# Hybrid decode step: memory values by tokens, norm weights on ScalarE, a shorter Newton step, selected-value loads one per step

## The chip, the core and the metric

The kernel runs on one core of a Trainium2 chip, as one launch. The metric is the device time of that launch in microseconds (us). Beside it stands the profile of one execution, taken by the hardware profiler. The core has five engines with a queue of instructions each: TensorE (PE; its weight loads are shown as PEld), VectorE (DVE), ScalarE (ACT), GpSimd (POOL) and SyncE (SP), which here only issues DMA transfers. GpSimd issues DMA transfers too, in the same queue as its arithmetic. An engine takes its own queue strictly in order; between engines, semaphores hold an instruction until its inputs are there and its output buffer is free.

## The reference

One layer of a decoder step over 256 prompt tokens and 8 × 4 = 32 decode tokens (288 columns in all), width 2048, float32:

```python
h = rms_norm(x, norm_g)                       # x * rsqrt(mean(x^2) + eps) * g
c_h, c_b, c_c, c_g, q, n_g, b_g, kv6, m_q, m_g = split_cols(h @ w_in)
y_a = silu(c_g) * short_conv(c_h, c_b, c_c)   # 512 channels
y_b = silu(n_g) * (g0 * o_cmp + g1 * o_sel + g2 * o_win)   # 8 heads, compressed / selected / window
mkv = rms_norm(mem_prompt, mem_norm_g) @ w_mem_kv          # 256 memory tokens: keys, values of 4 heads
y_m = silu(m_g) * attend(m_q, mkv or cache_mem)
y = rms_norm(x + concat(y_a, y_b, y_m) @ w_out, final_g)
```

The decode tokens attend to a paged cache of 2048 positions, of which the compressed branch picks 16 blocks of 64. Outputs are y, the new keys and values, the window and convolution states, and the memory keys and values.

## The kernel before, in words

**Layout.** Activations stand with channels on the 128 partitions and tokens along the free axis: x as 16 planes of 128 × 288, the memory prompt as 16 planes of 128 × 256. A product of the projections is 128 output channels by all tokens. Its weights come in two *halves*, tiles of 128 × 1024 (eight k-blocks of 128). For precision, weights and activations are each split into a high part (fp32r, by a ScalarE copy, `w_hi`) and a low part (what is left, by a VectorE subtraction, `w_lo`), and a half takes 24 matmuls: high × high, high × low, low × high for eight blocks (`product_half`, line 250). Halves are numbered `s`: 0 to 15 the memory projection, 16 to 119 `w_in`, and then `w_out`. At the start of half `s` the code puts `w_hi(s + 2)` on ScalarE and `w_lo(s + 1)` on VectorE; at matmul 21 of the half it issues the weight load of half `s + 6` (on GpSimd's queue from half 14) and, early on, one of the six loads of x (`x_next`).

**Order.** The order of work is written out by the program. All side work is Python generators in a list; after every 12 matmuls `chunk()` (line 161) advances each generator that is due by one step, so that its instructions are put in the queues between those matmuls. A generator yields the number of steps it wants to rest. A planner keeps an estimated clock for each engine (`at`) and uses it to hold work back (`until`, `ready`, `BACKLOG`); it only decides the order. `stages` (line 717) lists the cache work with due times in steps, `load_next` (line 731) fills six buffers of 128 × 1024 with the next loads on that list whenever buffers come free, and `stage_stream` uses them.

**Memory projection (22.5 to 60.7 us).** Tiles 0 to 3 are keys, 4 to 7 values, one tile per head. `mem_tile` (line 1016) brings a tile out of its result buffer: the keys by ScalarE, the values by VectorE times the token norm `rstd_m`, which is spread over all partitions. The result buffers are two (`pz`). Attention over the memory wants the values with tokens on the partitions, so `mem_rstd` (line 878) then transposes each value tile (two transposes on TensorE), copies both out by ScalarE and writes the tile to `o_mem`.

**x.** `prep_x` (line 930) multiplies each of 16 planes by the norm weight `g` (per partition) and the token factor `r` in one VectorE operation, three planes at a time; then ScalarE rounds the three planes to the high part and VectorE subtracts the low part. The x products, from half 16 on, need the parts.

**Selected values.** `selv_load` (line 583) fetches 128 rows of the value cache by an indirect DMA on GpSimd's queue. A stage (`selv_use`) takes four of them; there are eight stages, four for each half of the decode batch. `load_next` issues the loads as soon as buffers are free, up to four in a row. GpSimd's other work is half of the product of the compression (`cmp_use`, line 350): VectorE multiplies the key half of a tile, GpSimd the value half once VectorE's is done, and VectorE sums both later (`pooled`).

**Memory part of the output projection.** `split_y1` (line 1390) splits the mixed activations for `w_out`; it asks at each step whether the decode tokens' memory attention is there (`mem_decoded`), and splits that part then.

**Tail.** The last four column blocks of the output are computed with tokens on the partitions: two groups of 128 prompt tokens (`z[0]`, `z[1]`) and the 32 decode tokens (`zd`, `decode_rows`). For each group `squares` adds the residual on VectorE and sums the squares on ScalarE; `factors` calls `rsqrt` (line 199): a square root on ScalarE, then five small VectorE operations (the argument `v`, a reciprocal, and one Newton step in three); `spread_rows` spreads the factor by a matmul (`rb`), and `scale_rows` and `scale_tiles` scale and store.

Of the kernel before, what the change touches and what calls it, by code (L numbers as in the profile page):

```python
# [79 lines left out]
def decode_step(ctx, tc, xT, xN, xD, xL, fgl, memT, cst, w_in, w_mem, w_out, w_bg, pt, ptv, ckc, ckk, ckv, wk, wv, mk, mv,  # L80
                o_y, o_kv, o_mem, o_conv, o_wk, o_wv):
# [117 lines left out]
    def rsqrt(r, ssq, rest=None):  # L199

        v, t = small(3, "yv", 1)[:, :r.shape[1]], small(3, "yt", 1)[:, :r.shape[1]]
        act.activation(r, ssq, AF.Sqrt, scale=1.0 / D, bias=C("eps") if rest is None else rest)
        if rest is None:
            vec.tensor_scalar(v, ssq, 1.0 / D, EPS, op0=ALU.mult, op1=ALU.add)
        else:
            vec.scalar_tensor_tensor(v, ssq, 1.0 / D, rest, op0=ALU.mult, op1=ALU.add)
# [43 lines left out]
    def product_half(out, hi, lo, first, last):  # L250
# [10 lines left out]
        for n, (_, a, b) in enumerate(mm):  # L261
            if s == DIRECT and n == 0:
                w_load(s + WR)
            if n == LOAD_AT:
                w_load(s + WR + 1)
                next(x_next, None)
            matmul(out, a, b, start=(first and n == 0), stop=(last and n == 23))
            if n == 23 and LOW_FIRST <= s < NH - 18:
                w_lo(s + 2)
            if n % 12 == 11 and not (last and n == 23):  # L270
                chunk()
# [3 lines left out]
    def first_tiles():  # L275
# [3 lines left out]
        for k0 in (0, 8):  # L279
            for i in range(2):  # L280
# [23 lines left out]
                if k0 == 8:  # L304
                    yield z[i]

# [374 lines left out]

    def mem_out():
# [13 lines left out]
        env["mem_decoded"] = True  # L696

# [31 lines left out]
    nl = [0]  # L729

    def load_next():
# [14 lines left out]
    def stage_stream():  # L746
# [3 lines left out]
        for due, f, u, j in stages:  # L750
# [3 lines left out]
            if u is cmp_use:  # L754
                last_cmp = at[0]
            yield from u(j, tiles_of.pop((u, j)))
# [14 lines left out]
    rstd_m = Vc  # L771
    rstd_x = zt("C", "rstd_x")
# [22 lines left out]
    x_next = x_loads()  # L795

# [81 lines left out]
    def mem_rstd():  # L878
# [7 lines left out]
        yield from token_rstd(rstd_m, [macc[:, 0:256]], 256, 1)  # L886
        env["rstd_m"] = True
        for i in range(8):
            while i not in mem_raw:
                yield 1  # L890
            dst = mem_raw[i]
            if i < 4:
                vec.tensor_tensor(dst, dst, rstd_m, op=ALU.mult)
            yield 1
            if i == 3:
                nc.gpsimd.dma_start(o_mem[0:4].rearrange("m p n -> p m n"), mkT)
            if i >= 4:
                nc.gpsimd.dma_start(o_mem[i], dst)
                yield 2
                t = ptr.tile([128, 512], F32, name=f"mvtp{i}", tag="t")  # L900
                for s in range(2):
                    transpose(t[:, s * 128:(s + 1) * 128], dst[:, s * 128:(s + 1) * 128], ident)
                for s in range(2):
                    act.activation(mvn(s, i - 4), t[:, s * 128:(s + 1) * 128], AF.Copy)
# [3 lines left out]
    def token_rstd(dst, planes, n, lag):  # L908
# [9 lines left out]
        r = small(3, "yr")  # L918
# [11 lines left out]
    def prep_x():  # L930

        g, r = C("ng"), rstd_x
# [83 lines left out]
    def mem_tile(i, z):  # L1016
        dst = mkT[:, i, :] if i < 4 else zt("A", "mvt")[:, :256]
        if i < 4:
            act.activation(dst, z, AF.Copy)
        else:  # L1020
            yield 2
            assert "rstd_m" in env
            vec.tensor_tensor(dst, z, rstd_m, op=ALU.mult)
        mem_raw[i] = dst
# [102 lines left out]
    def mem_gate(h, z):  # L1127
# [3 lines left out]
        vec.tensor_scalar(sg_m[:, h, :], sg[:, 256:NT], 0.5, None, op0=ALU.mult)  # L1131

# [227 lines left out]
    for i in range(2, 8):  # L1360
        then(mem_tile(i, proj(*m_hl, 256)))

# [25 lines left out]
    y1 = {}  # L1388

    def split_y1():  # L1390
# [11 lines left out]
        while not env.get("mem_decoded"):  # L1402
            yield 1
        m = mixed[:, 4:8, 256:NT]
        vec.tensor_tensor(m, m, sg_m, op=ALU.mult)
# [356 lines left out]
```

## Time and profile before

| What | Value |
|---|---|
| median of 3 runs | 612.21 us (610.86 to 616.13) |
| the profiled execution | 616.16 us, of which 614.4 are the span from its first to its last instruction |
| mean granted TensorE clock | 0.996 |
| moved by DMA | 190.85 MB, on average 311 GB/s |
| median of 12 weight loads of w_mem, issue to landing | 7.1 us |

How to read the rows that follow. A row of the timeline gives the start in us from the span's start, the duration, the engine (SPq, POOLq: DMA issues), the line, the operation, output <- inputs by their names in the program, the shape, how many were merged (x16), and in square brackets how long the engine had been idle and who ended that. A helper records most operations, so their line is that of the helper (L120 matmul, L125 transpose, L137 VectorE and ScalarE); the names tell them apart. A row of a group gives the count, then busy us, the mean of one in ns, and the idle time before them. A row by windows gives the window and its length in us, then the busy us of PE, PEld, DVE, ACT and POOL with counts, the granted clock, the DMA share and GB/s. A row of waits gives the total in us, the number of times, and the longest. A plain float32 matmul or transpose with 128 columns shows as one or two passes; matmuls overlap, so what one costs is read from start to start.

### The profile page before, as it was taken

How to read it: one execution, taken by the hardware profiler on the slowest of the kernel's cores; microseconds unless marked ns; L12 is line 12 of the kernel's file. 1: busy time of each engine (PE TensorE's matmuls, PEld its weight loads, DVE VectorE, ACT ScalarE, POOL GpSimd, SP SyncE). 2: the span in 40 equal slices, each digit the busy share in tenths (PEclk: the TensorE clock that was granted, in tenths of full speed). 3: DMA queues.
4: the chain of work that ended last, by engine and by line, in shares of the span. 5: the costliest groups of instructions: out<-in, count | busy, mean ns of one | idle time of the engine just before them, and what ended most of it. 6: DMA issues, size and time to landing. Idle time of an engine off the chain costs nothing.

```text
span 614.4 us, 13419 instructions
## 1 busy us (share of the span) xinstructions
PE 603.0 (98%) x4919; PEld 554.0 (90%) x4919; DVE 461.0 (75%) x749; ACT 285.3 (46%) x499; POOL 200.5 (33%) x282
## 2 busy tenths in 40 slices
PE   8999999999999999999999999999999999999997
PEld 5999999989799999989889889899889989889995
DVE  4879899988485779989789888897668733357666
ACT  4755445543355444435334434543543544335552
POOL 2012544533124442433453552323111336222200
PEclk8999999999999999999999999999999999999999
DMA  8999798999968999798878898999899998859834
GB/s 285 394 403 404 258 320 300 345 310 337 365 203 280 370 407 375 250 387 298 310 232 313 284 386 273 309 318 311 289 334 332 336 353 291 288 195 411 281 130 155
DMA packets 76226, 190.85 MB, mean 311 GB/s; under 512 B 8896, under 2 KB 26464, under 8 KB 75904
## 3 DMA queue, kind: packets, MB, share of 16 engines
q0 software_dynamic: 26048, 100.48, 46.0%
q1 hardware_dynamic: 49104, 88.25, 40.4%
q10 hardware_dynamic: 1008, 1.25, 0.6%
q8 instruction: 39, 0.64, 0.4%
q14 instruction: 27, 0.22, 0.1%
HBM read 184.74 MB, written 13.60 MB: 323 GB/s over the span
## 4 chain that ended last, share of the span: by engine, by line
PE 78%; DMA 11%; DVE 8%; issue 2%; SPq 1%; ACT 0%; ACTq 0%; DVEq 0%
PE z L120 56%; DMA st<-ckc 5%; PE zr L120 4%; PE od L120 3%; DMA st<-ckk 3%; PE sk L120 3%; PE zf L120 2%; DVE wl L137 2%; DVE pooled L137 2%; PE acc L120 2%; PE s L120 2%; DMA rx<-xT 1%; DVE st L137 1%; PE pt L125 1%; DMA mraw<-memT 1%
## 5 line engine op out<-in xcount | busy, mean ns | idle before, releaser
L120 PE MATMUL z<-x,wh 128*128 128x288 f32 x1664 | 254.4, 302 | 0.0
L137 DVE TENSOR_TENSOR wl<-w,wh 128x1024 fp32r<-128x1024 f32 x147 | 185.7, 1265 | 84.6 <-PE z L120 34.9
L120 PEld LDWEIGHTS z<-x,wh 128*128 128x128 f32 x1664 | 229.7, 188 | 7.8 <-issue 6.1
L137 ACT ACTIVATE wh<-w 128x1024 fp32r<-128x1024 f32 x148 | 154.3, 1052 | 25.1 <-PE z L120 15.4
L120 PE MATMUL z<-x,wl 128*128 128x288 f32 x832 | 127.2, 295 | 0.3 <-DVE wl L137 0.3
L120 PEld LDWEIGHTS z<-x,wl 128*128 128x128 f32 x832 | 115.7, 188 | 0.8 <-DVE wl L137 0.7
L356 POOL TENSOR_TENSOR st<-st,cst 128x512 f32<-128x512 f32 x63 | 69.3, 1102 | 133.8 <-DVE st L137 49.3
L225 POOL DMA_DIRECT2D w<-w_in x104 | 58.2, 560 | 109.1 <-DVE wl L137 82.4
L137 DVE TENSOR_REDUCE pooled<-st 128x16 f32<-128x1024 f32 x63 | 76.2, 1210 | 5.8 <-POOL st L356 5.8
L137 DVE TENSOR_TENSOR st<-st,cst 128x512 f32<-128x512 f32 x63 | 43.3, 688 | 10.9 <-DMA st<-ckc 10.8
L225 POOL DMA_DIRECT2D w<-w_out x32 | 17.5, 550 | 63.0 <-DVE wl L137 43.1
L584 POOL DMA_INDIRECT st<-ckv,rows_v x26 | 27.1, 1042 | 31.9 <-PE od L120 17.4
L137 ACT ACTIVATE P<-P,nm 128x128 f32<-128x128 f32 (+1 forms) x32 | 14.2, 445 | 29.3 <-DVE nm L137 29.3
L120 PE MATMUL z<-m,wh 128*128 128x256 f32 x192 | 27.3, 287 | 0.5 <-DVE mvt L137 0.5
L120 PE MATMUL z<-y,wh 128*128 128x288 f32 x192 | 27.6, 297 | 0.0
L120 PE MATMUL z<-y1a,wh 128*128 128x288 f32 x168 | 26.7, 299 | 0.0
L120 PEld LDWEIGHTS z<-y,wh 128*128 128x128 f32 x192 | 26.3, 188 | 0.1
L120 PEld LDWEIGHTS z<-y1a,wh 128*128 128x128 f32 x168 | 23.6, 188 | 2.1 <-issue 1.2
L120 PEld LDWEIGHTS z<-m,wh 128*128 128x128 f32 x192 | 24.7, 191 | 0.8 <-issue 0.7
L120 PE MATMUL sk<-st,qz 128*32 128x256 f32 x272 | 20.4, 383 | 1.4 <-DMA st<-ckk 1.2
L120 PE MATMUL od<-st,S 128*32 128x256 f32 x256 | 18.7, 382 | 0.0
L120 PE MATMUL zf<-mixed,w 128*128 128x256 f32 x64 | 16.6, 421 | 1.9 <-DVE mixed L137 1.7
(318 smaller groups left out, 716.2 us busy)
## 6 DMA issues: line engine op xcount, KB each, us to landing
w<-w_in POOLq DMA_DIRECT2D x104, 512.0 KB
st<-ckc SPq DMA_DIRECT2D x126, 256.0 KB, 5.8
w<-w_out POOLq DMA_DIRECT2D x32, 512.0 KB
st<-ckk SPq DMA_DIRECT2D x112, 128.0 KB, 5.1
w<-w_mem SPq DMA_DIRECT2D x12, 512.0 KB, 7.1
o_wk<-wk POOLq DMA_DIRECT2D x8, 512.0 KB
o_wv<-wv POOLq DMA_DIRECT2D x8, 512.0 KB
st<-mv SPq DMA_DIRECT2D x7, 512.0 KB, 7.9
```

What stands on the lines that cost most here:

```text
L120: nc.tensor.matmul(out, a, b, **kw)
L125: nc.tensor.transpose(out, a, b)
L137: return getattr(self.engine, name)(*args, **kw)
L225: (nc.gpsimd if s >= ON_SYNC else nc.sync).dma_start(raws[s], wsrc[s])
L356: done.append(eng.tensor_tensor(tm[:, :, kv], tm[:, :, kv], acmp[:, kv].unsqueeze(1).unsqueeze(1).to_broadcast([128, 2, 4, 64]), op=ALU.mu ...
L584: nc.gpsimd.indirect_dma_start(t, None, ckv, bass.IndirectOffsetOnAxis(ap=rows_v[:, j * 4 + b:j * 4 + b + 1], axis=0))
```

## The change

Five things change.

1. **Memory values by tokens.** `mem_values` takes the place of four value tiles. The memory activations are the stationary operand and 512 value columns of the weights the moving one, so the results (two buffers, 128 tokens each) have tokens on the partitions: eight halves of 12 matmuls of 512 columns. ScalarE brings each result out once, times the token factor (`mr`, per partition), and the transposes and their copies are gone. The value weights lie in memory accordingly, and the values have an output of their own, written in two transfers. The steps (`chunk`) are as many as before.
2. **Norm weights by ScalarE.** `x_scales` multiplies the planes of one load of x by `g` on ScalarE, one load in each of the halves 7 to 12; `prep_x` multiplies a whole load by the token factor in one VectorE operation.
3. **Newton step in two operations**, in the three factors of the tail: the argument is formed already times −0.5 (`rest` gets three more columns, by one operation ahead).
4. **Decode residual by TensorE.** The residual of the 32 decode tokens is added to `zd` by a matmul with the identity ahead of `decode_rows`; `squares` and `gains` read the result buffer.
5. **Selected-value loads one per step.** In stages 0 to 2 of eight, load `n` = 1, 2, 3 of a stage is issued by a generator: `n` steps later in stages 0 and 1, one step later in stage 2. The planner's `ready` time is set as before. Besides, the memory part of `split_y1` is called by `mem_out` itself when the rest of the split is done.

```diff
     def rsqrt(r, ssq, rest=None):
...
+        if rest is not None:
+            act.activation(r, ssq, AF.Sqrt, scale=1.0 / D, bias=rest[0])
+            vec.scalar_tensor_tensor(v, ssq, -0.5 / D, rest[1], op0=ALU.mult, op1=ALU.add)
+            vec.reciprocal(r, r)
+            vec.scalar_tensor_tensor(t, r, r, v, op0=ALU.mult, op1=ALU.mult)
+            vec.scalar_tensor_tensor(r, t, 1.5, r, op0=ALU.add, op1=ALU.mult)
+            return
...
+    def run_half(s, mm, last, between=None):
+        m = len(mm) // 2
+        for n, (out, a, b, start, stop) in enumerate(mm):
...
+            if n == LOAD_AT * m // 12:
                 w_load(s + WR + 1)
                 next(x_next, None)
+                if s > 5:
+                    next(x_scale, None)
+            matmul(out, a, b, start=start, stop=stop)
...
+            if n == 7 and between:
+                between()
+            if n == m - 1:
+                chunk()
+            if n == 2 * m - 1 and not last:
                 chunk()
...
+    def mem_values():
+        z = [pz.tile([128, 512], F32, name=f"zv{tt}", tag="z") for tt in range(2)]
+        def out(tt):
+            planes = mixed[:, 12 + 2 * tt:14 + 2 * tt, 0:256]
+            act.activation(planes, z[tt].rearrange("p (a n) -> p a n", a=2), AF.Copy, scale=mr[:, tt:tt + 1])
+            nc.gpsimd.dma_start(o_memv[tt].rearrange("p (a n) -> p a n", a=2), planes)
+        for h in range(8):
+            s = nhalf[0]
+            nhalf[0] += 1
+            w_hi(s + 2)
+            w_lo(s + 1)
+            wh, wl = his.pop(s), los.pop(s)
+            mm = []
+            for tt in range(2):
+                for k in range(2):
+                    hi, lo = (m_hl[n][:, 2 * h + k, tt * 128:(tt + 1) * 128] for n in range(2))
+                    w = slice(k * 512, (k + 1) * 512)
+                    early = 2 * tt + (k if h == 7 and tt else 0)
+                    mm += [(early, tt, hi, wh[:, w]), (early, tt, lo, wh[:, w]), (2.5 if h == 7 and not tt else 4, tt, hi, wl[:, w])]
+            mm.sort(key=lambda x: x[0])
+            i = [[n for n, x in enumerate(mm) if x[1] == tt] for tt in range(2)]
+            run_half(s, [(z[tt], a, b, h == 0 and n == i[tt][0], h == 7 and n == i[tt][-1]) for n, (_, tt, a, b) in enumerate(mm)],
+                     h == 7, (lambda: out(0)) if h == 7 else None)
+        out(1)
+        chunk()
...
     def load_next():
...
-            f(j, n, t)
+            if f is selv_load and j < 3 and n:
+                spawn(begin(f, u, j, n, t), n if j < 2 else 1)
+            else:
+                f(j, n, t)
...
+    def x_scales():
+        for i in range(6):
+            yield
+            k, t = xg[i]
+            for j in range(t.shape[1] // NT):
+                act.activation(xr[k + j], xr[k + j], AF.Copy, scale=C("ng")[:, k + j:k + j + 1])
...
     def prep_x():
...
-                for j in range(k, k + n):
-                    vec.scalar_tensor_tensor(xr[j], xr[j], g[:, j:j + 1], r, op0=ALU.mult, op1=ALU.mult)
+                xv = x.rearrange("p (k n) -> p k n", n=NT)
+                vec.tensor_tensor(xv, xv, r.unsqueeze(1).to_broadcast([128, n, NT]), op=ALU.mult)
...
-    for i in range(2, 8):
+    for i in range(2, 4):
         then(mem_tile(i, proj(*m_hl, 256)))
+    mem_values()
...
+    vec.tensor_scalar(rest[:, 3:6], ssq[:, 0:3], -0.5 / D, -0.5 * EPS, op0=ALU.mult, op1=ALU.add)
...
+    matmul(zd[:, :128], ident, part[2], start=True, stop=False, skip_group_check=True)
     decode_rows(0, SPREAD_AT)
```

More of the change, by code (lines that the diff above doesn't have):

```diff
@@ L260, in product_half @@
         mm.sort(key=lambda x: x[0])
-        for n, (_, a, b) in enumerate(mm):
+        run_half(s, [(out, a, b, first and n == 0, last and n == 23) for n, (_, a, b) in enumerate(mm)], last)
+    def run_half(s, mm, last, between=None):
+        m = len(mm) // 2
+        for n, (out, a, b, start, stop) in enumerate(mm):
             if s == DIRECT and n == 0:
                 w_load(s + WR)
-            if n == LOAD_AT:
+            if n == LOAD_AT * m // 12:
                 w_load(s + WR + 1)
                 next(x_next, None)
-            matmul(out, a, b, start=(first and n == 0), stop=(last and n == 23))
-            if n == 23 and LOW_FIRST <= s < NH - 18:
+                if s > 5:
+                    next(x_scale, None)
+            matmul(out, a, b, start=start, stop=stop)
+            if n == 2 * m - 1 and LOW_FIRST <= s < NH - 18:
                 w_lo(s + 2)
-            if n % 12 == 11 and not (last and n == 23):
+            if n == 7 and between:
[3 more added lines that the diff above has]
+            if n == 2 * m - 1 and not last:
                 chunk()
@@ L696, in mem_out @@
         env["mem_decoded"] = True
+        if "rest" in y1:
+            while env.get("gated", 0) < 4:
+                yield 1
+            y1["rest"]()
     def window_copies():
@@ L755, in stage_stream @@
                 last_cmp = at[0]
+            assert all((u, j, n) in begun for n in range(pieces(u)))
             yield from u(j, tiles_of.pop((u, j)))
@@ L771, in decode_step @@
     rstd_m = Vc
+    mr = one.tile([128, 2], F32, name="mr")
     rstd_x = zt("C", "rstd_x")
@@ L885, in mem_rstd, with token_rstd @@
         yield 3
-        yield from token_rstd(rstd_m, [macc[:, 0:256]], 256, 1)
+        yield from token_rstd(rstd_m, [macc[:, 0:256]], 256, 1, mr)
         env["rstd_m"] = True
-        for i in range(8):
+        for i in range(4):
             while i not in mem_raw:
                 yield 1
-            dst = mem_raw[i]
-            if i < 4:
-                vec.tensor_tensor(dst, dst, rstd_m, op=ALU.mult)
+            vec.tensor_tensor(mem_raw[i], mem_raw[i], rstd_m, op=ALU.mult)
             yield 1
[L895 to L904, printed above, removed]
+        nc.gpsimd.dma_start(o_mem.rearrange("m p n -> p m n"), mkT)
     GROUPS = ((0, 0), (128, 0), (160, 96))
-    def token_rstd(dst, planes, n, lag):
+    def token_rstd(dst, planes, n, lag, r):
         groups = [x for x in GROUPS if x[0] + 128 <= n]
@@ L1016, in mem_tile @@
     def mem_tile(i, z):
[L1017 to L1024, printed above, removed]
+        act.activation(mkT[:, i, :], z, AF.Copy)
+        mem_raw[i] = mkT[:, i, :]
+        return
+        yield
     cos, sin = C("cos"), C("sin")
@@ L1401, in split_y1, with rest @@
             vec.tensor_tensor(y1["lo"](j)[:, :n], mixed[:, j, :n], y1["hi"](j)[:, :n].bitcast(F32), op=ALU.subtract)
[L1402 to L1405, printed above, removed]
-        act.activation(a[:, 4:8, 256:NT], m, AF.Copy)
-        for lo, j in ((a[:, 12:14, 256:NT], 4), (b[:, :, 256:NT], 6)):
-            vec.tensor_tensor(lo, mixed[:, j:j + 2, 256:NT], a[:, j:j + 2, 256:NT].bitcast(F32), op=ALU.subtract)
-        y1["done"] = True
+        def rest():
+            m = mixed[:, 4:8, 256:NT]
+            vec.tensor_tensor(m, m, sg_m, op=ALU.mult)
+            act.activation(a[:, 4:8, 256:NT], m, AF.Copy)
+            for lo, j in ((a[:, 12:14, 256:NT], 4), (b[:, :, 256:NT], 6)):
+                vec.tensor_tensor(lo, mixed[:, j:j + 2, 256:NT], a[:, j:j + 2, 256:NT].bitcast(F32), op=ALU.subtract)
+            y1["done"] = True
+        y1["rest"] = rest
+        if env.get("mem_decoded"):
+            rest()
     spawn(split_y1(), 2)
@@ L1530, in decode_step @@
     out = (yo[:, 0:2048], yo[:, 2048:4096], yod)
-    rest, sums2 = small(3, "yrest", 1), small(3, "ysums", 1)
+    rest, sums2 = small(6, "yrest", 1), small(3, "ysums", 1)
     quarters = small(32, "imp", 1)
```

54 lines of the change are left out of this document (32 added, 22 removed).

## The prediction

> **What bounds the kernel now.** I read the page's head first, then the busy time by stage, then what TensorE (PE) waited for.
>
> ```profile
> span 614.4 us, 13419 instructions
> PE 603.0 (98%) x4919; PEld 554.0 (90%) x4919; DVE 461.0 (75%) x749; ACT 285.3 (46%) x499; POOL 200.5 (33%) x282
> ...
> 30.00:45.00 15.00, 15.00 (x125) 14.69 (x124) 10.57 (x27) 9.18 (x16) 2.42 (x4) 1.00 1.03 404
> 45.00:60.00 15.00, 14.50 (x121) 14.33 (x120) 15.00 (x24) 8.80 (x14) 3.76 (x7) 1.00 1.04 403
> ...
> 150.00:165.00 15.00, 13.63 (x115) 11.62 (x114) 8.67 (x11) 6.99 (x15) 2.69 (x4) 1.00 1.03 382
> ```
>
> TensorE is busy 603.0 of 614.4 us, at full clock (1.00) in the stages shown. The memory projection runs from 22.5 to 60.7 us; in its second part, 45 to 60, VectorE (the third figure, 15.00) has no free time, ScalarE (8.80) has 6.2 us free, and the DMA share is full (1.04). So the change can give time in two ways only: less work on TensorE, or fewer of its waits. These are short:
>
> ```profile
> PE sk L120 <- DMA st<-ckk: 1.2, 1, 1.2
> PE pt L125 <- DVE P L137: 1.2, 1, 1.2
> ...
> PE z L120 <- DVE mvt L137: 0.5, 1, 0.5
> PE rb L120 <- DVE yr L137: 0.4, 1, 0.4
> ```
>
> The third and fourth are waits that the change takes up by construction; the second lies among the selected-value loads; the first is a wait for cache pages, late by DMA.
>
> **Part 1: memory values by tokens.** Now four tiles of 128 value columns take 2 halves of 24 matmuls of 256 columns each; then come 8 transposes and 8 small evictions. After it, 8 halves have 12 matmuls of 512 columns, with no transposes and two evictions.
>
> ```profile
> 39.15 1.99 PEld L120 LDWEIGHTS z<-m,wh 128*128 128x128 f32 x16
> 42.03 1.99 PEld L120 LDWEIGHTS z<-m,wh 128*128 128x128 f32 x16
> 47.79 1.51 PEld L120 LDWEIGHTS z<-m,wh 128*128 128x128 f32 x12
> 50.88 1.99 PEld L120 LDWEIGHTS z<-m,wh 128*128 128x128 f32 x16
> 54.59 1.66 PE L120 MATMUL z<-m,wh 128*128 128x256 f32 x12 [0.50 <-DVE mvt L137]
> L125 PE MATMUL mvtp<-cst,mvt 128*128 128x128 f32 x8 | 1.5, 272 | 0.0
> ...
> 592.39 0.88 PEld L120 LDWEIGHTS zr<-wh,y 128*128 128x128 f32 x4
> 593.79 0.88 PEld L120 LDWEIGHTS zr<-wh,y 128*128 128x128 f32 x4
> ```
>
> From start to start, a half of 24 narrow matmuls lasts 42.03 − 39.15 = 2.88 us; one that holds two transposes 50.88 − 47.79 = 3.09, so a pair of transposes costs 0.21. Matmuls of 512 columns stand at the end of the kernel: six from 592.39 to 593.79, 1.40 us, so twelve 2.80. The terms: 8 × (2.88 − 2.80) = 0.64; four pairs × 0.21 = 0.84; the wait of 0.50 for VectorE to empty a result buffer (mvt) has no successor, as the two new results stay in place until the last half. Together **2.0 us** less on TensorE. The last half finishes the first result four matmuls early, so that ScalarE can empty it under 4 × 0.23 = 0.9 us of other matmuls, and the branch-gate matmuls follow before the buffer is needed: no cost.
>
> **Part 2: norm weights by ScalarE.** Sixteen planes of x get their weight by a ScalarE multiplication, three planes in a half; VectorE then multiplies three planes in one instruction.
>
> ```profile
> L137 ACT ACTIVATE wh<-w 128x1024 fp32r<-128x1024 f32 x8 | 8.4, 1047 | 0.0
> L137 DVE SCALAR_TENSOR_TENSOR rx<-rx,cst,rstd_x 128x288 f32<-128x288 f32 x16 | 7.4, 512 | 0.0
> L137 DVE TENSOR_TENSOR x<-rx,x 128x864 fp32r<-128x864 f32 x5 | 5.3, 1050 | 0.0
> L137 ACT ACTIVATE x<-rx 128x864 fp32r<-128x864 f32 x5 | 4.6, 928 | 7.9 <-DVE rx L137 7.9
> L137 DVE TENSOR_TENSOR mvt<-z,Vc 128x256 f32<-128x256 f32 x3 | 1.2, 415 | 0.0
> ...
> L137 ACT ACTIVATE ysum<-ysum,cst 128x288 f32<-128x288 f32 x12 | 6.4, 537 | 0.4
> ```
>
> VectorE loses 7.4 us and gets five wide and one narrow product, at most 5 × 1.05 + 0.45 = 5.7 (a subtraction over the same three planes took 1.05); the mvt products (0.42 each) go too. So its queue is relieved by some 3.4 us where it is full. ScalarE gets 16 multiplications: the same form at the end of the kernel took 0.54, so 8.6 us, in the halves from about 34 to 50 us. In one half it then has 1.05 (rounding of the weights) + 0.93 (rounding of x) + 1.61 = 3.59 us against 2.80 on TensorE. It falls 0.8 us behind per half, four halves long: 3.2 us late. Weights are rounded two halves ahead, so 2 × 2.80 − 1.05 = 4.55 us may pass before TensorE waits; but the engines now wait on each other (product on scaling, rounding on product, subtraction on rounding, the next low weights behind it). Least 0 of lost time, most 4.0 (five halves, no lead at all). I take **0.5 lost**, nearer the lower end, because 3.2 is under 4.55.
>
> The Trainium skill (ScalarE: Activation LUTs, What ACT_TABLE_LOAD costs) puts such a multiplication at about 186 + 93 + 0.833 × 288 = 519 ns, with neighbours overlapping by 93; the row of 537 agrees with the first. With the overlap a half would need 3.3 us instead of 3.59, nothing would be lost, and the sum below would be 0.5 better.
>
> **Part 3: the tail.** One Newton operation less in each of three chains; the decode residual is added by an identity matmul on TensorE instead of VectorE.
>
> ```profile
> 601.72 0.30 PEld L120 LDWEIGHTS rb<-cst,yr 128*128 128x128 f32 x2 [0.35 <-DVE yr L137]
> 606.51 0.30 PEld L120 LDWEIGHTS rb<-cst,yr 128*128 128x128 f32 x2 [0.20 <-DVE yr L137]
> 607.86 0.29 DVE L137 TENSOR_TENSOR ysum<-zd,ysum 128x128 f32<-128x128 f32 x1
> 608.07 0.68 DVE L137 TENSOR_TENSOR yo<-ysum,rb 128x512 f32<-128x512 f32 x1
> 608.19 0.31 ACT L137 ACTIVATE st<-ysum 128x128 f32<-128x128 f32 x1 [1.18 <-DVE ysum L137]
> 609.06 0.26 ACT L137 ACTIVATE yr<-ssqy,yrest 128x1 f32<-128x1 f32 x1 [0.47 <-PE ssqy L120]
> 609.47 0.15 DVE L137 SCALAR_TENSOR_TENSOR yv<-ssqy,yrest 128x1 f32<-128x1 f32 x1
> ...
> 609.91 0.16 DVE L137 SCALAR_TENSOR_TENSOR yt<-yt,yv 128x1 f32<-128x1 f32 x1
> 610.11 0.16 DVE L137 SCALAR_TENSOR_TENSOR yr<-yt,yr 128x1 f32<-128x1 f32 x1
> ...
> 167.06 1.78 PE om L120 x16
> ```
>
> A dependent small VectorE operation takes 610.11 − 609.91 = 0.20 us. In chain 1 TensorE waits 0.35 for the factor and would wait 0.15: 0.2 earlier. Then the identity matmul adds two passes of 1.78 / 16 = 0.11, that is 0.22; so the decode rows start no earlier, but chain 2's factor is there before TensorE asks, and its wait of 0.20 goes: 0.2 in all so far. In chain 3 the square starts on the finished sum, 608.19 − 607.86 = 0.33 earlier, which with the 0.2 puts the end of the square root at 608.8 instead of 609.06 + 0.26 = 609.32. VectorE's queue gets to yv 0.6 sooner, at about 608.85: 0.2 for the shift, 0.2 for the sum that left it (608.07 − 607.86), 0.2 for the wait for that sum. Then comes one Newton operation less, 0.2; in all up to 0.8. The additional VectorE operation on the partial sums lies under the second z group. I take **0.7 us**, near the upper bound as both queues were followed; the lower is 0.2, if chain 3 is then held by something else.
>
> **Part 4: selected-value loads.** Before, four indirect loads are issued in one burst; after, in three of the eight stages, one per scheduler step.
>
> ```profile
> 292.58 1.25 POOL L584 DMA_INDIRECT st<-ckv,rows_v  x1 [2.91 <-PE od L120]
> 296.65 0.94 POOL L584 DMA_INDIRECT st<-ckv,rows_v  x1 [0.30 <-issue]
> 297.61 1.10 POOL L356 TENSOR_TENSOR st<-st,cst 128x512 f32<-128x512 f32 x1
> ...
> 297.01 2.79 DVE L137 TENSOR_TENSOR wl<-w,wh 128x1024 fp32r<-128x1024 f32 x1 [4.11 <-ACT wh L137]
> 306.83 1.47 DVE L137 TENSOR_TENSOR P<-P,sm 128x512 f32<-128x512 f32 x1
> 308.44 0.63 PE L125 MATMUL pt<-cst,P 128*128 128x128 f32 x4 [1.17 <-DVE P L137]
> ```
>
> The burst holds GpSimd (POOL) from 292.58 to 297.59, so its compression product starts at 297.61, 4.7 us after VectorE's half, right under the next low-weight subtraction, which takes 2.79 instead of the 1.21 at 308.22. The queue behind it is 1.6 us late; the softmax product P at its end is met by the next GpSimd product, and TensorE waits 1.17. With one load per step, GpSimd's product runs between two loads, when VectorE was idle for the rounding anyway. Gain between 0 (the stall comes from another overlap) and 1.17; I take **0.65**, the middle, since the P product was itself stretched by GpSimd work that isn't an indirect load. The landing is safe: a stage is read some 15 us after its last issue, and three steps move it by about 5.
>
> The Trainium skill (SBUF — State Buffer, SBUF: two separate sides) says VectorE with two SBUF inputs and a GpSimd operation that reads SBUF exclude each other for a whole instruction. The row of 2.79 agrees, and the rule cuts both ways: nine loads apart have nine chances to hold VectorE. By it alone this term would be 0.
>
> **Elsewhere.** The decode part of the memory output is now split for the output projection as soon as it exists; no row of TensorE's waits names it, so 0. At 158 us TensorE waits 1.2 for cache pages while the DMA share is 1.03: what comes sooner there waits longer, between 0 and the 1.5 gained by then. Page loads are issued when buffers come free, which moves along with the compute, so I take **0.4 given back**.
>
> **Sum.** 2.0 − 0.5 + 0.7 + 0.65 − 0.4 = 2.45 us less than the profiled execution's 616.16. The median of the runs is 612.21; I take the same 2.45 off it: **609.8 us**, 0.4% faster. About 1% (6.1 us) is what a measurement of this kernel can tell from no change, as its own runs lie between 610.86 and 616.13.
>
> **Rivals.**
> (A) The relief does more: nothing is lost in part 2, the whole 1.17 of part 4 goes, and the pages come sooner too, as their buffers come free sooner, so that the 1.2 at 158 us goes. For it: the stretched rows of part 4, and 15.00 of 15 busy in part 2. Against it: the full DMA share. 2.0 + 0.7 + 1.2 + 1.2 = 5.1: 607.1.
> (B) The pages are the bound: all of 2.0 is waited away at 158 us, and the spread loads bring nothing; the tail alone stays, 0.7: 611.5. For it: share 1.03. Against it: only one such wait.
> (C) Slower: ScalarE becomes the bound from 34 to 56 us. Its price is 4.0, as above, plus what the low weights behind it wait, 0.2 in each of five halves: 5.0; against 2.0 + 0.7 that is 2.3 slower, 614.5 with nothing from part 4. It decides once ScalarE is over 4.55 us late. The Trainium skill (ScalarE: Activation LUTs, Rules for kernel authors) speaks for this one: it wants plain multiplications on VectorE.
> (D) The spread doesn't do what it says: nine loads are moved, but GpSimd's product still lands under the same subtraction. 609.8 + 0.65 = 610.45.
>
> **Chances.** Forecast 0.45 (its own range 608 to 611.3), A 0.18, B 0.14, C 0.13, D 0.10. The range that leaves 2 in 10 out reaches from a little under A to short of C: 606.6 to 613.6. Faster by over 1% means under 606.1: about half of A's spread, plus the scatter of the runs, 0.12. Slower by over 1% means over 618.3: the far end of C, 0.05. The rest, 0.83, lies within 1%.
>
> **What would show it.** Right: no mvtp rows; memory halves 2.80 us apart; the first x matmul 1 to 2 us sooner than 62.78; the two rb waits of 0.35 and 0.20 down to about 0.16 and 0; single indirect loads with GpSimd products between, and the subtraction near 297 back to 1.2; from the last zd matmul to the last DMA issue 0.4 shorter. Wrong: TensorE waiting on wh or wl between 40 and 60; a wait for pages at 158 longer than 2; new DMA waits in 300 to 350 on od; the pt wait still there.

## The result, and the profile after

The kernel after takes 609.84 us (median of 22 runs, 608.37 to 612.66), the kernel before, run beside it, 612.55 (22 runs, 610.86 to 620.05). The ratio is 0.9949, 95% interval 0.9935 to 0.9964 (the two medians alone give 0.9956): 0.4 to 0.5% faster, within 1%. The forecast was 609.8. The sum came out right, in part by luck: three of its five terms did not, a fourth stays open, and the experiments show which.

The profiled execution of the kernel after took 608.97 us. First the head of its page.

```profile
span 607.1 us, 13202 instructions
PE 600.1 (99%) x4817; PEld 547.5 (90%) x4817; DVE 454.2 (75%) x732; ACT 292.2 (48%) x509; POOL 203.4 (34%) x280
```

TensorE does 2.9 us less work (603.0 − 600.1) in a span that is 7.3 us shorter, so more than half of the difference between these two executions is not work that went but time in which TensorE had none. This pair overstates the gain: the profiled execution of the kernel before took 616.16 us, 3.6 above its median, that of the kernel after 0.9 less than its own. Next the busy time by stage, the stages of the prediction:

```profile
30.00:45.00 15.00, 15.00 (x87) 13.02 (x86) 11.58 (x25) 12.00 (x23) 2.98 (x5) 1.00 1.03 401
45.00:60.00 15.00, 14.96 (x75) 11.69 (x78) 14.66 (x17) 13.31 (x19) 4.04 (x8) 1.00 1.04 404
150.00:165.00 15.00, 15.00 (x131) 13.70 (x130) 8.10 (x10) 7.35 (x14) 3.28 (x6) 1.00 0.91 316
```

From 45 to 60 us ScalarE has gone from 8.80 to 13.31 us, and VectorE is still at 14.66: the relief was filled again. From 150 to 165 TensorE has no gap left (before 13.63). The waits of TensorE, all that the view lists:

```profile
PE zf L120 <- DVE mixed L137: 1.2, 2, 1.0
PE zeros L120 <- POOL zeros L892: 1.2, 1, 1.2
PE z L120 <- DVE wl L137: 0.4, 1, 0.4
PE rb L120 <- DVE yr L137: 0.2, 1, 0.2
PE z L120 <- ACT wh L137: 0.2, 1, 0.2
```

The waits for cache pages (sk, 1.2), for the softmax product (pt, 1.2) and for the emptied buffer (mvt, 0.5) are gone. To see where the time went, I took from the timeline of TensorE the start of every half of weights (24 narrow or 12 wide matmuls) and subtracted. "After, again" is a second profiled execution of the same kernel (e9 below).

| Stretch | before, us | after, us | after, again, us |
|---|---|---|---|
| start to half 6 (first loads) | 28.47 | 27.50 | 28.78 |
| half 6 to 24 (rest of the memory stage, first x halves) | 61.34 | 59.60 | 59.62 |
| half 24 to 34 | 32.00 | 32.00 | 32.00 |
| half 34 to 42 (first key stage) | 30.04 | 29.88 | 30.56 |
| half 42 to 50 (second and third key stage) | 39.15 | 36.71 | 36.92 |
| half 50 to 64 | 51.81 | 52.16 | 52.15 |
| half 64 to 82 (first selected-value loads) | 81.08 | 78.99 | 79.06 |
| half 82 to 150 | 273.50 | 273.63 | 273.55 |
| half 150 to the end | 17.02 | 16.61 | 16.60 |

Four rows are shorter by more than the scatter of the second column against the third: the memory stage (1.74 less), the second and third key stage (2.44 less), the selected-value loads (2.09 less) and the tail (0.41 less). The row from half 50 to 64 is 0.35 longer, but e1 to e4 below, each the kernel before with one part of the change, take 52.10 to 52.45 there, so it is the one execution of the kernel before that is short. The first row is not the change's: half 6 stands between 27.45 and 29.40 us in the fourteen profiles of this study, for the kernel after at 27.50 and at 28.78, and everything behind moves along.

The largest of the four was not in the forecast. It lies at the second of the key stages (the expectations below count it as the third). Before, as the timeline of TensorE shows it:

```profile
156.75 2.21 PE L120 MATMUL sk<-st,qz 128*32 128x256 f32 x22
160.20 1.02 PE L120 MATMUL sk<-st,qz 128*32 128x256 f32 x10 [1.24 <-DMA st<-ckk]
161.15 0.66 PE L125 MATMUL ptm<-cst,Pm 128*128 128x128 f32 x4
```

and after:

```profile
156.16 1.82 PE L120 MATMUL z<-x,wh 128*128 128x288 f32 x12
157.92 1.93 PE L120 MATMUL sk<-st,qz 128*32 128x256 f32 x32
159.78 2.05 PE L120 MATMUL om<-PTm,mixed 128*128 128x128 f32 x16
```

Before, the 32 score matmuls take from 156.75 to 161.15, 4.40 us, in two pieces with a wait for a page between them; after, 157.92 to 159.78, 1.86 us in one piece. And it is not the same place in the program: before, the stage stands in the middle of half 43, after in the middle of half 44. Nothing in the diff says so. The planner moved it. Its own clock for TensorE, `at[0]`, counts less for the wide memory halves; it spaces the compression steps by that clock, so the last of them falls one half later, and the key stages, which queue behind, do too. The reason is read from the planner's rules; that part 1 moves the stage is shown by e1 below, which has part 1 alone and the stage at half 44, while e2, e3 and e4 have it at half 43. What the move is worth is the matter of two more experiments.

### The profile page after: what moved, and what is told of

It reads as the page before. It is cut to its first block, busy times and chain, and to the rows that moved or that the text cites. A ratio compares the mean times of both kernels' runs of the same rounds, so it can differ in the third digit from the quotient of the medians.

```text
span 607.1 us, 13202 instructions
## 1 busy us (share of the span) xinstructions
PE 600.1 (99%) x4817; PEld 547.5 (90%) x4817; DVE 454.2 (75%) x732; ACT 292.2 (48%) x509; POOL 203.4 (34%) x280
## 4 chain that ended last, share of the span: by engine, by line
PE 93%; DVE 3%; DMA 2%; ACT 1%; issue 0%; ACTq 0%; SPq 0%; DVEq 0%
PE z L120 68%; PE zr L120 4%; PE zv L120 4%; PE od L120 3%; PE sk L120 3%; PE acc L120 2%; PE s L120 2%; DMA st<-xD 1%; PE pt L125 1%; DMA mraw<-memT 1%; PE pv L125 1%; PE om L120 1%; PE omd L120 1%; PE smd L120 1%; PE zf L120 1%; DVE wl L137 1%
## 5 line engine op out<-in xcount | busy, mean ns | idle before, releaser
L137 DVE TENSOR_TENSOR wl<-w,wh 128x1024 fp32r<-128x1024 f32 x147 | 183.4, 1250 | 79.0 <-PE z L120 44.0
L401 POOL TENSOR_TENSOR st<-st,cst 128x512 f32<-128x512 f32 x56 | 62.2, 1111 | 103.5 <-DVE st L137 58.5
L137 DVE TENSOR_REDUCE pooled<-st 128x16 f32<-128x1024 f32 x56 | 67.9, 1212 | 4.5 <-POOL st L401 4.4
L137 DVE TENSOR_TENSOR st<-st,cst 128x512 f32<-128x512 f32 x56 | 38.3, 685 | 6.8 <-DMA st<-ckc 6.8
L629 POOL DMA_INDIRECT st<-ckv,rows_v x29 | 31.5, 1087 | 33.4 <-PE od L120 11.6
L137 ACT ACTIVATE se<-z 128x288 f32<-128x288 f32 x16 | 6.5, 408 | 30.7 <-PE z L120 30.7
L137 ACT ACTIVATE ysum<-z 128x288 f32<-128x288 f32 x12 | 5.0, 413 | 26.6 <-PE z L120 26.6
```

Source lines behind the costliest of these rows:

```text
L137: return getattr(self.engine, name)(*args, **kw)
L401: done.append(eng.tensor_tensor(tm[:, :, kv], tm[:, :, kv], acmp[:, kv].unsqueeze(1).unsqueeze(1).to_broadcast([128, 2, 4, 64]), op=ALU.mu ...
L629: nc.gpsimd.indirect_dma_start(t, None, ckv, bass.IndirectOffsetOnAxis(ap=rows_v[:, j * 4 + b:j * 4 + b + 1], axis=0))
```

## The experiments

The theory after this profile: (1) the memory stage gave what it did because VectorE, not ScalarE, bounds it, so part 2 is a gain; (2) the page wait went because the planner moved the key stages; (3) the tail is worth 0.4; (4) the spread loads by themselves bring nothing, since the stall they were to cure stands in some executions only. The rivals: the scales cost time and part 1 alone would be better; the pages themselves came sooner; the loads are what removed the pt wait.

**Each part alone on the kernel before.** Four kernels: part 1 with the earlier split of the memory output; part 2; the tail (Newton step and identity matmul); the spread loads. Their diffs are the corresponding pieces of the change's diff, nothing else.

> The kernel before with the memory values by tokens alone (and the memory part of the split called by mem_out). Theory (TensorE's work is the gain): halves of 12 wide matmuls last 2.72 us instead of 2.88, no transposes, no wait for mvt; but norm weights stay on VectorE, so the low weights are late there: 1.3 to 2.6 us faster. Rival (the gain is a re-roll of the page wait at 158 us and of the softmax wait at 307): within 0.7 us of the kernel before, or faster by over 3. Of the profile: wide halves 2.72 us apart; ScalarE without the 8.6 us of scaling.

> The kernel before with the norm weights by ScalarE alone. Theory (ScalarE is the bound of that stage, and VectorE had just enough time before): between 0.3 faster, as the wait of 0.50 for mvt goes, and 0.8 slower, as the low weights come late. Rival (VectorE was the bound of the stage, and its relief is what gives the time): 0.5 to 1.5 us faster, first x matmul earlier by that much.

> The kernel before with the shorter Newton step and the residual by TensorE alone. Theory (from the trace after: the tail from the last z group on is 0.43 us shorter, as the second factor is no longer waited for but the identity matmul costs 0.25 to 0.3, and a Newton operation that takes two scalars from memory took 0.22 instead of 0.16): 0.3 to 0.6 us faster, all of it after 590 us. Rival (prediction): 0.7 faster. Rounds may not tell 0.4 from 0.7; the profile's rows can.

> The kernel before with the selected-value loads of stages 0 to 2 one per step alone. Theory (bursts hold GpSimd, its product lands under the next subtraction, and the softmax row behind is late): 0.5 to 1.5 us faster; in the profile the subtraction near 297 us takes 1.2 instead of 2.79, and TensorE's wait for P near 308 is gone. Rival (the P wait comes from another overlap or is there in some executions only): within 0.3 us of the kernel before, the wait still there or replaced by another.

Measured, with the kernel before in the same group at 613.46 us (35 runs, 610.95 to 617.58):

| Kernel | Median, us | Ratio to before | 95% interval |
|---|---|---|---|
| e1, memory values by tokens | 611.80 | 0.9974 | 0.9953 to 0.9995 |
| e2, norm weights by ScalarE | 614.77 | 1.0004 | 0.9973 to 1.0035 |
| e3, tail | 612.91 | 0.9992 | 0.9963 to 1.0021 |
| e4, spread loads | 613.42 | 1.0006 | 0.9985 to 1.0028 |

Only e1 can be told from no change by its time. The profiles say more. In e1 the halves 6 to 24 take 60.68 us, only 0.66 less than before, though the wide matmuls and the lost transposes should give more. Its timeline of TensorE shows who takes it back:

```profile
49.14 1.97 PE L120 MATMUL zv<-wh,m 128*128 128x512 f32 x8
51.50 1.20 PE L120 MATMUL zv<-wl,m 128*128 128x512 f32 x4 [0.39 <-DVE wl L137]
52.54 1.98 PE L120 MATMUL zv<-wh,m 128*128 128x512 f32 x8
54.90 1.21 PE L120 MATMUL zv<-wl,m 128*128 128x512 f32 x4 [0.38 <-DVE wl L137]
55.94 1.55 PE L120 MATMUL zv<-wh,m 128*128 128x512 f32 x6
```

A half now lasts 52.54 − 49.14 = 3.40 us. The kernel after has the same half in 2.72 where nothing waits (46.41 − 43.69 in its timeline). The low weights, which VectorE makes, are late in both halves: 0.68 us lost in each. In e2 the same stretch takes 60.58 us, 0.76 less than before: the relief of VectorE is a gain even with the narrow matmuls. But then:

```profile
PE sk L120 <- DMA st<-ckk: 2.2, 1, 2.2
PE zf L120 <- DVE mixed L137: 1.7, 2, 1.0
```

What came sooner waited longer for the page, 2.2 instead of 1.2 us, and its time is that of before. That fits rival B of the prediction, but one execution does not show it: e3, with the same order and the memory stage of before, has 0.3. In e1 there is no sk wait; the planner has moved the stage to half 44, as in the kernel after, so the 1.7 us by which e1 is faster hold more than its memory stage. e3 takes 16.58 us from half 150 to the end (before 17.02), so the tail is worth 0.44 on its own. e3 also says something on the pt wait: it still has the burst of four loads, and no pt wait; its subtraction beside the burst took 1.23 us, not 2.79. So the stall that I had priced from one execution is not in every execution.

**The order alone.** Two kernels with no change of work. The planner's test for a stage was shifted for the first three key stages, later on the kernel before (+1.5), sooner on the kernel after (−2.5):

```diff
-  or at[0] < ready[u, j]
+  or at[0] < ready[u, j] + (1.5 if u is selk_use and j < 3 else 0)
```

> Kernel before with one addition: the planner takes the first three selected-key stages only 1.5 us of its own clock after they are ready, so the third one falls one half later (44.5 instead of 43.5), as in the kernel after. No work is changed. Theory (the wait for cache pages at 158 us vanishes from the kernel after because the stage stands one half later): no sk wait on a DMA at 150 to 165 us, 1.0 to 1.8 us faster than before (the wait took 1.2, 2.2, 2.1 and 0.3 us in the profiles with the early order, 1.45 on the mean), ratio near 0.9977. Rival (the pages come sooner because of the shorter memory stage, and the place of the stage is idle): the wait stays near 1 us, ratio 0.999 to 1.001.

> Kernel after with one addition: the planner takes the first three selected-key stages 2.5 us of its own clock sooner, so they stand at halves 37 and 43.5 as in the kernel before. Theory (order): the sk wait on a DMA comes back with 1 to 2.5 us, and the kernel is 1.0 to 2.0 us slower than the one after, some 611.1 against 609.8, ratio to before near 0.9975. Rival (sooner pages): no wait over 0.5 us, ratio 0.995 as the kernel after.

Measured beside the kernel before at 615.07 us (23 runs, 611.36 to 621.20): e5 613.95, ratio 0.9977 (0.9954 to 0.9999); e6 619.78, ratio 1.0086 (1.0058 to 1.0115). e5 does what the theory said. Its second key stage:

```profile
161.53 1.93 PE L120 MATMUL sk<-st,qz 128*32 128x256 f32 x32
163.39 2.05 PE L120 MATMUL om<-PTm,mixed 128*128 128x128 f32 x16
```

One piece, 1.86 us, as after: the wait is gone from the kernel before, with the same work and no shorter memory stage; the stage came later, at 161.53 instead of 156.75. The shift moves all of the first three stages, and the third from half 49 to half 50, so work passes from one row of the table to the next. Over halves 42 to 64 together e5 takes 88.7 us; the four profiles with the order of before (before, e2, e3, e4) take 89.9 to 92.3, the eight with that of after (after, e1, e7 to e12) 88.9 to 89.5. So the order is worth 2.1 us there on the mean of the profiles.

The rival that the pages come sooner is not excluded for the kernel after. By the landing times in the traces the last page of this stage landed at 156.53 us in that kernel and at 158.30 in e1, while the wait of the kernel before ended at 160.20. One half takes 3.20 us (the row of half 34 above). The stage starts at 157.92 us in the first and at 159.07 in e1. One half sooner it would have come to that page, 22 matmuls of 0.058 us in, at some 156.0 and 157.2 us. An estimate from these figures leaves 0.5 and 1.1 us of waiting. So in e1 it is the order that saves the wait, and in the kernel after the order and pages that landed sooner share it.

e6 went the way of the theory in its sign, but neither in size nor in place. Its time is 9 us above e7 and e8 of the same group (the kernel after with small changes, below), where 1 to 2 were expected. And the stage at half 43, where the wait was to come back, has none; other stages have. Its waits, that stage, and its granted clock, from the waits of TensorE, its timeline and the busy time by stage:

```profile
PE sk L120 <- DMA qk<-ckk: 4.6, 1, 4.6
PE sk L120 <- DMA st<-ckk: 1.9, 1, 1.9
PE otm L125 <- DVE odr L137: 1.1, 1, 1.1
```

```profile
156.87 1.93 PE L120 MATMUL sk<-st,qz 128*32 128x256 f32 x32
```

```profile
205.00:212.00 7.00, 7.00 (x61) 6.61 (x63) 4.23 (x5) 2.58 (x4) 2.54 (x5) 1.00 1.03 358
212.00:218.00 6.00, 1.43 (x33) 0.72 (x25) 0.00 (x0) 0.00 (x0) 0.00 (x0) 1.00 1.03 400
218.00:226.00 8.00, 8.00 (x67) 7.62 (x60) 4.61 (x9) 3.01 (x8) 3.81 (x5) 0.79 0.90 339
226.00:234.00 8.00, 8.00 (x62) 8.00 (x61) 7.52 (x19) 3.22 (x4) 3.60 (x6) 1.00 0.93 303
```

The first stage waits 1.9 us, the fourth, which my shift does not name, 4.6. After the 4.6 the clock granted to TensorE is 0.79 for 8 us (the third row, last but two figures), another 8 × 0.21 = 1.7 us. Another 5.0 us lie from half 82 to 150 (278.66 us, the kernel after 273.63), where the later stages stand at other halves too; why these cost as much was not followed. So e6 is not the kernel after in the order of before. It shows that an order alone can cost 9 us, not what that one stage is worth. e5 is the cleaner measure: 1.1 us by the medians, with an interval from 0.1 to 2.8.

**Part 2 on top of part 1.** The kernel after with the norm weights given back to VectorE, and the kernel after with the scales begun one half earlier (`if s > 5:` became `if s > 4:`), run in the group of e5 and e6.

> Kernel after without the norm weights by ScalarE: VectorE multiplies with weight and factor again. Theory (VectorE was the bound of the memory stage, and its relief is worth 0.76 alone and 1.1 on top of the memory values by tokens): 0.9 to 1.3 us slower than the kernel after, waits for wl of about 0.8 and 0.4 at 50 to 55 us, ratio to before 0.9964 to 0.9972. Rival of the prediction (the scales cost 0.5 us): 0.3 to 0.8 us faster than the kernel after, ratio near 0.994.

> Kernel after with the norm-weight scales begun one half earlier (first at half 5 of the loop instead of 6). Theory (in the last memory halves VectorE, held by the scaled planes that come late from ScalarE, gives the low weights 0.46 and 0.33 us late): those two waits and part of the 0.28 for the last result go, 0.5 to 0.9 us faster than the kernel after, ratio to before 0.9935 to 0.9942. Rival (VectorE is full whatever the order, the sum of its work sets the waits): within 0.2 us of the kernel after, ratio 0.9946 to 0.9952. Third: the x planes have not landed that early and ScalarE waits for the DMA, which holds the rounding of weights behind it: slower than the kernel after.

Measured: e8 610.59, ratio 0.9912 (0.9879 to 0.9945); e7 610.49, ratio 0.9908 (0.9874 to 0.9941). The kernel before is slower in this group than in the first, so these ratios can't be set against 0.9949; I had expected ratios that hold across groups, and they don't. So e8 was run again beside the kernel after, with a third kernel. That one came from e7's profile: with the earlier scales the last memory halves wait no more, but the first scale had got ahead of the square root for the factor of x on ScalarE's queue, and TensorE then waited 0.7 us for that factor ("rx <- DVE yr"). Halves 6 to 24 took 60.11 us, 0.5 more than in the kernel after, which e7 was expected to beat by 0.5 to 0.9. So the third kernel leaves the first scale where it was and issues a second one at half 8:

```diff
                 if s > 5:
                     next(x_scale, None)
+                if s == 8:
+                    next(x_scale, None)
```

> The kernel after, unchanged, beside the three others of this group, so that they can be compared with it on one chip. Ratio to before 0.993 to 0.997 (it was 0.9949).

> The kernel after without the norm weights by ScalarE, again, this time beside the kernel after. Theory (VectorE bounds the memory stage; by the starts of the halves the relief is worth 1.1 us on top of the memory values by tokens): 0.7 to 1.5 us slower than the kernel after. Rival of the prediction (the scales cost 0.5 us): 0.3 to 0.8 us faster than it.

> The kernel after with a second scale of three planes issued at half 8 of the loop, so that from there on ScalarE is one half ahead of VectorE's products, and the square root for the factor keeps its place. Theory (the waits of 0.46, 0.33 and 0.28 us at 53 to 58 us come from VectorE waiting 0.17 us twice for a scaled plane): these waits go, the x product starts 0.7 to 1.1 us sooner, and the kernel is 0.6 to 1.1 us faster than the kernel after. Rival (the second scale pushes the rounding of weights or of x on ScalarE, as the early one pushed the square root): a new wait of 0.3 us or more at 38 to 50 us, within 0.3 us of the kernel after.

Measured, beside the kernel before at 617.05 us (13 runs, 613.66 to 621.77):

| Kernel | Median, us | Ratio to before | 95% interval |
|---|---|---|---|
| e9, the kernel after | 609.75 | 0.9886 | 0.9844 to 0.9928 |
| e10, without the norm weights by ScalarE | 611.53 | 0.9911 | 0.9879 to 0.9942 |
| e12, one scale of catch-up | 609.45 | 0.9882 | 0.9841 to 0.9923 |

The ratio of e9 lies outside the 0.993 to 0.997 expected, as the kernel before is slower again in this group.

Without part 2 the kernel is 1.8 us slower by the medians: the theory, a little over its range, and against the prediction's sign. The runs are few (8 and 6) and their ranges overlap; the means differ by 1.5 us, with a 95% interval of about 0.2 to 2.8. The profiles are firmer. In halves 6 to 24 e10 takes 60.75 us and e8, the same kernel, 60.73, against 59.60 and 59.62 for the kernel after: 1.13 more, with the two waits of e1 back at the same places:

```profile
52.82 1.20 PE L120 MATMUL zv<-wl,m 128*128 128x512 f32 x4 [0.39 <-DVE wl L137]
53.86 1.99 PE L120 MATMUL zv<-wh,m 128*128 128x512 f32 x8
56.22 1.21 PE L120 MATMUL zv<-wl,m 128*128 128x512 f32 x4 [0.37 <-DVE wl L137]
```

In the profiles another 0.5 us lies at the first key stage (31.04 us from half 34 to 42 against 30.56) and as much from half 42 to 50; the first differs by more than that between the two executions of the kernel after (29.88 and 30.56), so neither is put down to part 2. In e12 the last memory halves run without a gap, as the theory said. Its ScalarE, with six scales in a row, and its TensorE:

```profile
39.23 2.66 ACT L137 ACTIVATE rx<-rx,cst 128x288 f32<-128x288 f32 x6
```

```profile
53.75 1.98 PE L120 MATMUL zv<-wh,m 128*128 128x512 f32 x8
55.57 1.07 PE L120 MATMUL zv<-wl,m 128*128 128x512 f32 x4
56.47 1.53 PE L120 MATMUL zv<-wh,m 128*128 128x512 f32 x6
```

56.47 − 53.75 = 2.72. Halves 6 to 24 take 59.13 us, 0.5 less than the kernel after; I had expected 0.7 to 1.1, because I had added up idle times of the weight loads (0.46, 0.33), which run ahead and hide part of such a gap. By time it can't be told from the kernel after (609.45 against 609.75, ranges 608.81 to 610.56 and 608.72 to 611.40): a gain that the profile shows and these runs don't resolve.

**The tail in two.** The kernel after with the residual by VectorE again and the shorter Newton step kept, in one execution.

```diff
-    matmul(zd[:, :128], ident, part[2], start=True, stop=False, skip_group_check=True)
...
-    squares(2)
+    squares(2, zd[:, :128])
```

> The kernel after with the decode residual added by VectorE again, the shorter Newton step kept. From the start of half 150 to the end of the span the kernel after takes 16.61 us and the one before 17.02. Theory (the gain of 0.43 comes from the finished sum, the square starting 0.33 sooner, while the identity matmul's 0.22 cancels the shorter Newton step in chain 1): 16.8 to 16.95 us here. Rival (the Newton step alone brings it): 16.55 to 16.7.

It took 610.71 us, and 16.76 from half 150 to the end, a stretch that varies by 0.03 us at most among the profiles with the tail of before, and among those with that of after. Neither theory: of the tail's 0.42 (17.02 − 16.60) the identity matmul brings 16.76 − 16.60 = 0.16 and the shorter Newton step 17.02 − 16.76 = 0.26.

## Why the prediction was right, and where it was wrong

**Part 1, 2.0 us on TensorE: the mechanism right, the amount hidden at first.** A wide half takes 2.72 us, not 2.80: a 512-column matmul in it takes 0.227 us, in the tail rows from which I took it 1.40 / 6 = 0.233. So the terms are 8 × 0.16 + 0.84 + 0.50 = 2.6. Alone it gives 0.66 (e1), as the low weights are late; where nothing is late any more, in e12, the stretch is 61.34 − 59.13 = 2.2 shorter.

**Part 2, "0.5 lost": the wrong sign.** The step that failed is "It falls 0.8 us behind per half": I added ScalarE's durations and let it be the slower engine, though the row of 45 to 60 us had VectorE at 15.00 of 15. What the runs show is a relief of VectorE worth 0.76 us alone (e2) and 1.1 on top of part 1 (e10 against e9). A round of VectorE in the kernel before, from one low-weight subtraction to the next, took 55.33 − 51.60 = 3.73 us with a product of the values (mvt) in it and 3.39 without (48.21 to 51.60), while a half of TensorE takes 2.88. So VectorE was over TensorE's time already, and the sum had no term for its relief:

```profile
51.60 1.22 DVE L137 TENSOR_TENSOR wl<-w,wh 128x1024 fp32r<-128x1024 f32 x1
52.74 1.37 DVE L137 SCALAR_TENSOR_TENSOR rx<-rx,cst,rstd_x 128x288 f32<-128x288 f32 x3
54.03 0.41 DVE L137 TENSOR_TENSOR mvt<-z,Vc 128x256 f32<-128x256 f32 x1
54.36 1.05 DVE L137 TENSOR_TENSOR x<-rx,x 128x864 fp32r<-128x864 f32 x1
55.33 1.21 DVE L137 TENSOR_TENSOR wl<-w,wh 128x1024 fp32r<-128x1024 f32 x1
```

The kernel after shows the two engines at the same work, first ScalarE, then VectorE:

```profile
49.24 1.38 ACT L137 ACTIVATE rx<-rx,cst 128x288 f32<-128x288 f32 x3
50.52 1.05 ACT L137 ACTIVATE wh<-w 128x1024 fp32r<-128x1024 f32 x1
51.74 0.93 ACT L137 ACTIVATE x<-rx 128x864 fp32r<-128x864 f32 x1 [0.17 <-DVE rx L137]
```

```profile
49.26 1.22 DVE L137 TENSOR_TENSOR wl<-w,wh 128x1024 fp32r<-128x1024 f32 x1
50.65 1.06 DVE L137 TENSOR_TENSOR rx<-rx,rstd_x 128x864 f32<-128x864 f32 x1 [0.17 <-ACT rx L137]
51.62 1.05 DVE L137 TENSOR_TENSOR x<-rx,x 128x864 fp32r<-128x864 f32 x1
```

A round of VectorE now takes 52.59 − 49.26 = 3.33 us, where its next subtraction starts. Three scales took 1.38 us, not 1.61, so a half is 1.38 + 1.05 + 0.93 = 3.36 us for ScalarE. By the overlap of neighbours that the Trainium skill (ScalarE: Activation LUTs, What ACT_TABLE_LOAD costs) states, the prediction had worked out 3.3 for it; the row of 1.38 agrees. I had weighed the page against one row of the tail and left it out of the sum. What is left of my mechanism is small: VectorE waits 0.17 us for a scaled plane twice, and the last halves lose 0.5, which e12 takes away. Parts 1 and 2 together are 1.74 us in the table, 1.5 in the sum: two errors that nearly cancel.

**Part 3, 0.7: too high, 0.42.** "VectorE's queue gets to yv 0.6 sooner" holds by half: from the start of half 150, yv starts 12.08 us later in the kernel before (609.47 − 597.39) and 11.77 in the kernel after (602.24 − 590.47), 0.31 sooner. The 0.2 that chains 1 and 2 were to bring did not come. The decode rows start 6.25 us after half 150, where before it was 6.15. In the kernel after the identity matmul took 0.32 us, not 0.22, and the new Newton operation with two column operands takes 0.22 and passes its result on after 0.25, where the old one took 0.16 and 0.20:

```profile
602.50 0.22 DVE L137 SCALAR_TENSOR_TENSOR yt<-yr,yv 128x1 f32<-128x1 f32 x1
602.75 0.16 DVE L137 SCALAR_TENSOR_TENSOR yr<-yt,yr 128x1 f32<-128x1 f32 x1
```

```profile
596.40 0.38 PE L120 MATMUL zd<-ysum,cst 128*128 128x128 f32 x2
596.72 1.95 PE L120 MATMUL zd<-st,mixed 128*32 128x128 f32 x64
```

Of the two rb waits that I had named, the first fell from 0.35 to 0.22; the second is still 0.20, though no longer put down to VectorE, so the 0.2 that I had counted for it was not won.

**Part 4, 0.65: not resolved.** The loads of the kernel after are single, with GpSimd's products between them:

```profile
287.07 1.03 POOL L629 DMA_INDIRECT st<-ckv,rows_v  x1 [4.07 <-DVE st L137]
288.11 1.13 POOL L401 TENSOR_TENSOR st<-st,cst 128x512 f32<-128x512 f32 x1
...
290.07 1.00 POOL L629 DMA_INDIRECT st<-ckv,rows_v  x1 [0.30 <-issue]
294.15 1.10 POOL L401 TENSOR_TENSOR qk<-qk,cst 128x512 f32<-128x512 f32 x1 [3.08 <-issue]
```

and the subtractions beside them take 1.22 us. But the pt wait is 1.2, 0, 0, 1.5 and 0.5 us in the five profiles with the burst (before, e2, e3, e5, e1), 0.64 on the mean, and 0 in the nine with single loads. From half 64 to 82 the five take 79.13 to 81.37 us, 80.26 on the mean; those with single loads take 78.99 to 79.41, 79.12 on the mean (e6 left out, whose stages stand elsewhere). So the 2.09 us of the table is one execution, and the profiles put the part at 1.1. The timed run of the part alone (e4, 613.42 against 613.46) shows none of it; its interval, from 0.9 us faster to 1.7 slower, holds both 0 and 0.65. The step that was wrong is to take a stall of one execution for a property of the kernel. Whether the spread is worth a microsecond or nothing stays open.

**"0.4 given back" at the pages: the wrong sign.** The step took it that the stage stays where it is in the program and moves along with the compute. It did not stay: the planner put it one half later, and 1.2 us of waiting, 2.5 with the gap around it, went instead. e5 shows that this order is worth about 1 us on the kernel before. Whether my reasoning would have held with the old order is not settled. e2, with a sooner stage, waited longer (2.2 us); e3 waited 0.3 with nothing changed there; the stage of e6 at half 43 did not wait at all. So rival B ("the pages are the bound") may be at work in single executions; the new order avoids it.

**How firm the total is.** That the forecast was met to 0.04 us is luck. The terms as measured are 1.74 for parts 1 and 2, 0.42 for the tail, about 1.1 for the order and 0 to 1.1 for the loads, 3.3 to 4.4 together; the medians of the first group differ by 2.7, and the runs do not show where the rest went. The time of the kernel after repeats (609.84 and 609.75 us in two groups); that of the kernel before does not (612.55, 613.46, 615.07 and 617.05 in four), so that the ratio was 0.9949 in one group and 0.9886 in another, with intervals that don't overlap. e1 to e8 ran on one chip and e9 to e12 on another, but two of the four medians, 613.46 and 615.07, are of one chip. The part of the gain that hangs on waits for pages is the likeliest to vary so, since the sk wait alone was 0.3 to 2.2 us in the profiles with the old order; that it is what moves the medians was not shown. In the last group the forecast time is met too, but the gain is 1.1%, not under 1.

## What to carry to other kernels

Where a planner with a clock of its own writes the order, compare the order of the two programs first: every changed cost moves that clock, and a stage that moves by one half can be worth as much as the edit. Price a shift of work between two engines from the one that is full in that stage; time taken off it counts even if the other gets more to do than TensorE takes for the half. A stall seen in one execution is worth its mean over several executions, and the terms of a sum should say which kind they are.

## What the runs showed of the hardware

After the wait of 4.6 us in e6 the granted clock was 0.50 from 218.2 to 221.5 us (the 0.79 above is over 8 us), then 1.00 again. It was 0.50 from 494.7 to 498.0 us as well, right behind two waits of 0.9 and 1.1 us. After the wait of 1.2 us at 160 us in the kernel before, and of 1.9 us at 132 us in e6, it stayed at 1.00. So a gap on TensorE can cost more than its length. The Trainium skill (TensorE: Matmul & The Clock Gate, Part 1: The HAM clock gate) says that an idle window of about 3.4 us halves the clock until about as long a busy stretch has passed. The dip behind the 4.6 agrees in depth and in length. The second dip follows no idle stretch as long as that, and no run here shows why it came and why none came after the 1.9.

The same score matmuls on cache pages took 1.86, 2.6 and 3.1 us at the first key stage in three executions of kernels with the new order (32 matmuls, from their start to that of the next in after, e9 and e10). TensorE's matmul rows list no wait there; among its weight loads e9 has one of 0.4 us and e10 one of 0.3 for a page, and e10 one of 0.6 put down to nothing. So a stage can lose a microsecond while its pages land with hardly a row that says so.
